# Score products one level later in TensorE's order, behind the making of the next level's operands, in a gated-linear-attention and mixture-of-experts block

## Chip, cores and metric

The kernel runs on one core of one Trainium2 chip. The metric is device time in microseconds (us); lower is better.

## What is computed

One decoder block over 512 tokens of width 1024, in fp32. A projection of the normalised input feeds a convolution branch and a chunked gated linear attention (GLA); both are gated, added and projected; a mixture of 32 experts (top 2) and a final norm follow. The part that the change touches is the intra-chunk score of the GLA:

```python
diff = b[:, :, :, None, :] - b[:, :, None, :, :]
decay = jnp.exp(jnp.where(causal, diff, -jnp.inf))
attn = jnp.einsum("bhid,bhijd,bhjd->bhij", qc, decay, kc)
o_intra = jnp.einsum("bhij,bhje->bhie", attn, vc)
```

with `b` the running sum of the log gates (4 heads of 128 keys and 256 values).

## The kernel before

TensorE is PE, VectorE DVE, ScalarE ACT, GpSimd POOL, SyncE SP. The 512 tokens stand in four blocks of 128. Every large product is done as three fp32r passes over high and low parts of its operands. The weights are streamed in pieces: `piece` loads one (SP), rounds it to a high part on ACT (`hiw`, `hipw`, `higo`, L410) and subtracts on POOL or DVE to get the low part (`low`, `lopw`, `logo`, L384).

`scores(t)` makes the score matrix of block `t` in seven levels, `l` = 0 to 6. At level `l` pairs of neighbouring groups of 2^l tokens meet. DVE makes the difference `dd` of `b` to a reference row in two instructions, ACT its exponential `fac` (one PSUM bank, tag `bg`), DVE the product tile `m` of `fac` with keys and with queries in two instructions, PE the product `pl` (small matmuls on halves of the array), and DVE (levels 0 to 4, `copy_predicated`) or ACT (levels 5 and 6) puts the valid part into `attn`. `dd` and `m` have two buffers each, `pl` two banks (tag `g`).

The program is written in the order: convolution, values (`tm`, token-major), scores 0 and 1, read gate `r` (`tm`), block 0, scores 2 and 3, blocks 1 to 3, normalisation and transposes, first branch gate (`fmw`, evacuated to `yc`), convolution output product (`pw`), second branch gate (`fmw`, evacuated to `th`), GLA output product (`fmgo`), output product (`wo`), router, experts. But in this part of the program the engines' orders (except SP's, and from `wo` on PE's, DVE's and ACT's) are not the written ones: a scheduler with a timeline of its own lays them out, with the dependencies and with the extra order hints of `after(ins, other)`, which make no instruction wait and only say that `ins` is to be placed no earlier than `other` is done on that timeline.

`block(t)` multiplies `attn` and the state with the values into `po` (two banks, tag `tr`), and carries the state on (`kd`, `pk`, `kt`, `pst`, `st`). After block 3 the squares give `so` (square root on ACT, reciprocal on DVE), 16 DVE instructions scale `sr` by it, and for k = 0 to 7 PE transposes `sr` into `pot` (tag `tr`, two banks), ACT rounds to the high part and DVE subtracts for the low part (`ohl`, `olo`, L69). `fmgo` sums over k = 0 to 7 in each of its eight tiles, so its first tile needs all eight of them.

In the background DVE sums rows of the modulation weights (`acc_a`, `acc_b`, twice `acc_ga`, `acc_bf`, `acc_af`, 8 instructions each) from 1 MB transfers that ACT's queue issues into two buffers (`aw_...`).

Of the kernel before, what the change touches and what calls it, by code (L numbers as in the profile page):

```python
# [25 lines left out]
H = 4  # L26
# [34 lines left out]
def kernel(ctx: ExitStack, tc: tile.TileContext, a, dbg=None):  # L61
# [3 lines left out]
    def tt(out, in0, in1, op):  # L65
        return V.tensor_tensor(out, in0, in1, op=op)  # L66
# [12 lines left out]
    def after(ins, other):  # L79
        tc.add_manual_dep(raw_ins(ins), raw_ins(other).name, NOSYNC, reason="order")  # L80
# [483 lines left out]
    def scores(t):  # L564
# [12 lines left out]
        bf = b.rearrange("p h i -> p (h i)")  # L577
        kf = kb[t].rearrange("p h i -> p (h i)")
        qf = qb[t].rearrange("p h i -> p (h i)")
        for l in range(7):  # L580
            s = 1 << l
            m = H * P // (2 * s)
            half = lambda x: x.rearrange("p (m g s) -> p m g s", g=2, s=s)
            dd = tl("dd", f"dd{t}_{l}")
            ref = half(bf)[:, :, 0, s - 1:s].to_broadcast([P, m, s])
            tt(half(dd)[:, :, 0, :], ref, half(bf)[:, :, 0, :], ALU.subtract)
            tt(half(dd)[:, :, 1, :], half(bf)[:, :, 1, :], ref, ALU.subtract)

            fac = bank("bg", f"fac{t}_{l}")
            A.activation(fac, dd, AF.Exp)  # L590
            mm = tl("mm", f"m{t}_{l}", (P, H, P))
            mf = mm.rearrange("p h i -> p (h i)")
            tt(half(mf)[:, :, 0, :], half(fac)[:, :, 0, :], half(kf)[:, :, 0, :], ALU.mult)
            tt(half(mf)[:, :, 1, :], half(fac)[:, :, 1, :], half(qf)[:, :, 1, :], ALU.mult)

            pl = bank("g", f"pl{t}_{l}")
            if l == 6:
                for h in range(H):
                    T.matmul(pl[0:64, h * 64:(h + 1) * 64], mm[:, h, sides[0]], mm[:, h, sides[1]], start=True, stop=True, tile_position=(0, 0))
                A.copy(at[0:64, :, sides[1]], pl[0:64, 0:H * 64].rearrange("p (h i) -> p h i", h=H))  # L600
                continue
            if l == 5:
                for h in range(H):
                    for e in range(2):
                        T.matmul(pl[64 * e:64 * e + 32, h * 32:(h + 1) * 32], mm[:, h, 64 * e:64 * e + 32], mm[:, h, 64 * e + 32:64 * e + 64],
                                 start=True, stop=True, tile_position=(0, 64 * e))
# [12 lines left out]
    vt = [tl("v", f"v{t}") for t in range(NT)]
# [946 lines left out]
```

## Time and profile before

| | us |
|---|---|
| median of 3 runs | 1013.49 (1012.28 to 1017.1) |
| profiled execution, its own time | 1016.07 |
| span of its trace | 1014.4 |
| PE busy | 953.9 (94%) |
| DVE busy | 556.2 (55%) |
| ACT busy | 339.5 (33%) |
| POOL busy | 184.0 (18%) |

The profiled execution is 1016.07 us long, 1.7 us more than its span, and 2.6 us above the median. Busy shares are averages over stages that have different limits; a stage is read by the waits in it.

### The profile page before, as it was taken

The page shows a single profiled execution, that of the slowest core. Times are in us where ns is not written, and L with a number is a line of the kernel's source. Part 1 is how long each engine was busy: PE and PEld are TensorE (multiplying, and loading weights), DVE is VectorE, ACT ScalarE, POOL GpSimd, SP SyncE. Part 2 cuts the span into 40 slices and gives each one's busy share as a digit, 9 for nine tenths or more (in the row PEclk, how much of TensorE's full clock was granted, in tenths as well). Part 3 has the DMA queues.
Part 4 walks back from the last instruction along what each step waited for, and adds up shares of the span by engine and source line. Part 5 has one row for each costly group of instructions (what it writes and reads, how often), then busy time and mean ns, then how long its engine had stood idle before and what let it go on. Part 6 is the DMA issues. An engine that isn't in the chain of part 4 may idle for free.

```text
span 1014.4 us, 13547 instructions
## 1 busy us (share of the span) xinstructions
PE 953.9 (94%) x5170; PEld 612.9 (60%) x5170; DVE 556.2 (55%) x1039; ACT 339.5 (33%) x689; POOL 184.0 (18%) x122
## 2 busy tenths in 40 slices
PE   7999999999989999899999999999989999899993
PEld 4778899888768887687764353534435344344431
DVE  6768899888885898974441232323213232222436
ACT  7656323374136554433861101110110101101114
POOL 5513433322321111411220000000000000000005
PEclk9999999998999999999999999999999999999997
DMA  9863223214852678639659999999999999999952
GB/s 281 231 167 84 84 85 103 79 48 146 270 187 64 206 229 291 194 104 394 269 227 421 421 421 421 420 420 421 420 423 420 421 421 419 421 420 421 419 222 85
DMA packets 114344, 283.94 MB, mean 280 GB/s; under 512 B 10691, under 2 KB 77995, under 8 KB 90212
## 3 DMA queue, kind: packets, MB, share of 16 engines
q1 hardware_dynamic: 104636, 252.21, 65.3%
q10 hardware_dynamic: 7624, 27.27, 7.7%
q0 software_dynamic: 2016, 3.56, 0.9%
q8 instruction: 42, 0.69, 0.3%
q14 instruction: 26, 0.21, 0.1%
HBM read 282.61 MB, written 4.19 MB: 283 GB/s over the span
## 4 chain that ended last, share of the span: by engine, by line
PE 50%; DMA 22%; issue 9%; DVE 9%; POOL 5%; ACT 2%; SPq 2%; POOLq 0%; DVEq 0%; ACTq 0%
DMA p_w<-in_w 16%; PE pog L1391 8%; PE hag L1361 7%; PE hbg L1361 7%; PE fmw L393 6%; PE pcg L1436 5%; POOL low L384 4%; PE fmgo L393 3%; PE pw L393 2%; DMA adaw<-in_w_ada 2%; PE wo L262 2%; DVE dd L66 2%; PE wo L264 1%; PE wo L263 1%; DMA raww<-in_w_in 1%
## 5 line engine op out<-in xcount | busy, mean ns | idle before, releaser
L384 POOL TENSOR_TENSOR low<-raww,hiw 128x1024 fp32r<-128x1024 f32 x36 | 91.2, 2534 | 213.3 <-ACT hiw L410 213.3
L69 DVE SCALAR_TENSOR_TENSOR conv<-z,cols,conv 128x511 f32<-128x511 f32 (+14 forms) x120 | 88.6, 739 | 5.5 <-ACT conv L482 1.8
L393 PE MATMUL fmw<-uhi,hiw 128*128 128x512 f32 x224 | 90.3, 403 | 1.3 <-ACT hiw L410 0.8
L393 PE MATMUL fmw<-uhi,low 128*128 128x512 f32 x224 | 91.0, 406 | 0.0
L393 PE MATMUL fmw<-ulo,hiw 128*128 128x512 f32 x224 | 90.4, 404 | 0.0
L69 DVE SCALAR_TENSOR_TENSOR pog<-pog,wslg,ga2r 128x512 f32<-128x512 f32 (+1 forms) x33 | 24.5, 742 | 95.2 <-PE pog L1391 88.8
L393 PE MATMUL tm<-low,uhi 128*128 128x256 f32 x256 | 73.2, 287 | 0.0
L393 PE MATMUL tm<-hiw,uhi 128*128 128x256 f32 x256 | 73.0, 289 | 0.0
L393 PE MATMUL tm<-hiw,ulo 128*128 128x256 f32 x256 | 72.8, 286 | 0.0
L1436 PE MATMUL pcg<-ohlg,backg 128*128 128x512 f32 (+1 forms) x264 | 67.5, 404 | 5.2 <-DVE hx L66 4.1
L410 ACT CAST hiw<-raww 128x1024 fp32r<-128x1024 f32 x44 | 46.0, 1046 | 75.4 <-issue 41.8
L1436 PEld LDWEIGHTS pcg<-ohlg,backg 128*128 128x128 f32 x264 | 46.7, 189 | 23.3 <-DVE hx L66 11.1
L66 DVE TENSOR_TENSOR hx<-hx,pcg 128x512 f32<-128x512 f32 (+1 forms) x84 | 53.2, 659 | 12.9 <-PE pcg L1436 12.4
L393 PEld LDWEIGHTS tm<-low,uhi 128*128 128x128 f32 x256 | 49.1, 192 | 0.9 <-issue 0.5
L393 PEld LDWEIGHTS tm<-hiw,uhi 128*128 128x128 f32 x256 | 48.8, 192 | 0.8 <-issue 0.5
L393 PEld LDWEIGHTS tm<-hiw,ulo 128*128 128x128 f32 x256 | 49.2, 192 | 0.1
L393 PEld LDWEIGHTS fmw<-uhi,hiw 128*128 128x128 f32 x224 | 42.4, 189 | 11.2 <-ACT hiw L410 0.9
L393 PEld LDWEIGHTS fmw<-ulo,hiw 128*128 128x128 f32 x224 | 42.5, 190 | 9.9
L393 PEld LDWEIGHTS fmw<-uhi,low 128*128 128x128 f32 x224 | 42.5, 190 | 9.7
L1412 ACT CAST ohlg<-pog 128x512 fp32r<-128x512 f32 (+1 forms) x33 | 18.9, 572 | 78.7 <-DVE pog L69 78.7
L66 DVE TENSOR_TENSOR dd<-b 128x256 f32<-128x256 f32 x56 | 32.5, 624 | 0.4 <-ACT fac L590 0.2
L590 ACT ACTIVATE fac<-dd 128x512 f32<-128x512 f32 x28 | 16.8, 601 | 42.3 <-DVE m L66 42.2
(506 smaller groups left out, 1887.7 us busy)
## 6 DMA issues: line engine op xcount, KB each, us to landing
p_w<-in_w SPq DMA_DIRECT2D x188, 1024.0 KB, 19.9
raww<-in_w_in SPq DMA_DIRECT2D x44, 512.0 KB, 4.0
adaw<-in_w_ada SPq DMA_DIRECT2D x32, 256.0 KB, 5.5
aw_ga<-in_w_ada ACTq DMA_DIRECT2D x8, 1024.0 KB, 5.1
aw_a<-in_w_ada ACTq DMA_DIRECT2D x4, 1024.0 KB, 7.6
aw_b<-in_w_ada ACTq DMA_DIRECT2D x4, 1024.0 KB, 5.1
aw_bf<-in_w_ada_f ACTq DMA_DIRECT2D x4, 1024.0 KB, 5.9
rawgo<-in_w_gla_o SPq DMA_DIRECT2D x8, 512.0 KB, 4.9
```

Source lines behind the costliest of these rows:

```text
L66: return V.tensor_tensor(out, in0, in1, op=op)
L69: return V.scalar_tensor_tensor(out, in0, scalar, in1, op0=op0, op1=op1)
L262: mm(o, ahi, bhi, start=first, stop=False)
L263: mm(o, ahi, blo, start=False, stop=False)
L384: (V if turn[0] % LO_EVERY < lo_v[0] else G).tensor_tensor(lo, raw, hi.bitcast(F32), op=ALU.subtract)
L393: ins = T.matmul(*args, **kw)
L410: copy = A.copy(hi, raw)
L590: A.activation(fac, dd, AF.Exp)
L1361: T.matmul(o[64 * e:64 * e + 64, :], xts[0][:, k, q * P + 64 * e:q * P + 64 * e + 64], w[wn, e, k // 4][:, k % 4, :], start=(k == 0), stop ...
L1391: T.matmul(o[64 * e:64 * e + 64, :], ht[:, f, 64 * e:64 * e + 64], w["w2", e, f // 2][:, f % 2, c0:c1], start=(f == 0), stop=(f == 3), til ...
L1412: A.copy(ohl[:, 0, c0:c1], prods[c])
L1436: T.matmul(o, back[z][:, t * P:(t + 1) * P], res[z][:, i, c0:c1], start=(z == qs[0] and i == 0), stop=(z == qs[-1] and i == 1))
```

## The change

`scores` is cut into `factors(l)`, which makes `dd`, `fac` and `m` of a level, and `level(l, behind)`, which does its products and puts them into `attn`. Level 0's factors come first; then for each level the factors of the next level are written ahead of its products, and the first product of level `l` gets an order hint: it is to be placed behind the last DVE instruction of the factors of level `l + 1`. No instruction is added or removed, and no tile has more or fewer buffers. For level 6 there is no hint.

```diff
-        for l in range(7):
+        half = lambda x, s: x.rearrange("p (m g s) -> p m g s", g=2, s=s)
+        mms = {}
+
+        def factors(l):
+
             s = 1 << l
             m = H * P // (2 * s)
...
+            return tt(hm[:, :, 1, :], hf[:, :, 1, :], half(qf, s)[:, :, 1, :], ALU.mult)
+
+        def level(l, behind):
+
+            s = 1 << l
+            mm = mms[l]
+            start = []
+
+            def product(*args, **kw):
+                ins = T.matmul(*args, start=True, stop=True, **kw)
+                if behind is not None and not start:
+                    after(ins, behind)
+                start.append(ins)
+
 
             pl = bank("g", f"pl{t}_{l}")
...
+        factors(0)
+        for l in range(7):
+            level(l, factors(l + 1) if l < 6 else None)
```

The scheduler lays out everything behind the first moved product anew: PE's rows differ from the first products of block 0's scores to the first rows of `wo`, and so do DVE's, ACT's and some of POOL's in between; SP's are the same. Three places follow.

PE in the first branch gate, levels 1 and 2 of block 2's scores (`fmw` is the gate's product, `pl` a level's product, `m` its operands). Before:

```order
L393 MATMUL fmw_1_3224<-ulo,hiw_1_3220 128x512
L613 MATMUL pl_1_2664<-m_1_2661 64x32 x8
L613 MATMUL pl_2_2683<-m_2_2680 64x32 x8
L393 MATMUL fmw_1_3224<-uhi,low_1_3221 128x512
L393 MATMUL fmw_1_3224<-uhi,hiw_1_3220 128x512
```

and now:

```order
L393 MATMUL fmw_0_3257<-uhi,low_0_3254 128x512
L607 MATMUL pl_1_2672<-m_1_2650 64x32 x8
L393 MATMUL fmw_0_3257<-uhi,hiw_0_3253 128x512
L393 MATMUL fmw_0_3257<-ulo,hiw_0_3253 128x512
L393 MATMUL fmw_0_3257<-uhi,low_0_3254 128x512
```

Level 2's products no longer stand directly behind level 1's: 20 rows of `fmw` lie between them now, and as many ahead of most other levels; while `tm` runs it is about 21 rows. In the same way the scores of block 3, which stood among the last rows of the first gate, now stand among the rows of `pw`, and the last rows of block 3's `po`, which had 42 of the 192 rows of the second gate ahead of them, have 141.

PE at the transposes `pot` (the third of them, number 3056). Before it stood in the second gate, `fmw`:

```order
L393 MATMUL fmw_1_3888<-ulo,hiw_1_3858 128x512
L731 MATMUL pot_3056<-ident,sr_1320 128x128
L731 MATMUL pot_3056<-ident,sr_1321 128x128
L731 MATMUL pot_3056<-ident,sr_1322 128x128
L731 MATMUL pot_3056<-ident,sr_1323 128x128
L731 MATMUL pot_3064<-ident,sr_1320 128x128
```

and now behind the first row of `fmgo`'s first tile (4030):

```order
L393 MATMUL fmgo_4030<-ohl_3039,higo_4002 128x512
L752 MATMUL pot_3056<-ident,sr_1320 128x128
L752 MATMUL pot_3056<-ident,sr_1321 128x128
L752 MATMUL pot_3056<-ident,sr_1322 128x128
L752 MATMUL pot_3056<-ident,sr_1323 128x128
L393 MATMUL fmgo_4030<-ohl_3039,higo_4002 128x512
L393 MATMUL fmgo_4030<-ohl_3039,logo_4003 128x512
L393 MATMUL fmgo_4030<-ohl_3047,higo_4002 128x512
```

Six of the eight transposes stand inside that tile now, three rows of `fmgo` between one and the next; before it was two of them.

DVE at the same place, the last low parts of the transposed rows. Before:

```order
L69 SCALAR_TENSOR_TENSOR ohl_3063<-pot_3064,gq,ohl_3063 128x512
L384 TENSOR_TENSOR low_1_3960<-raww_1_3957,hiw_1_3959 128x1024
L69 SCALAR_TENSOR_TENSOR acc_bf<-aw_bf_3967,cact,acc_bf 128x1024 x2
L69 SCALAR_TENSOR_TENSOR olo_3072<-pot_3073,gq,ohi_3071 128x512
L69 SCALAR_TENSOR_TENSOR olo_3081<-pot_3082,gq,ohi_3080 128x512
L384 TENSOR_TENSOR logo_4062<-rawgo_4059,higo_4061 128x1024
```

and now:

```order
L69 SCALAR_TENSOR_TENSOR ohl_3063<-pot_3064,gq,ohl_3063 128x512
L69 SCALAR_TENSOR_TENSOR acc_bf<-aw_bf_3926,cact,acc_bf 128x1024
L69 SCALAR_TENSOR_TENSOR olo_3072<-pot_3073,gq,ohi_3071 128x512
L69 SCALAR_TENSOR_TENSOR acc_bf<-aw_bf_3926,cact,acc_bf 128x1024
L69 SCALAR_TENSOR_TENSOR olo_3081<-pot_3082,gq,ohi_3080 128x512
L69 SCALAR_TENSOR_TENSOR acc_bf<-aw_bf_3963,cact,acc_bf 128x1024
L69 SCALAR_TENSOR_TENSOR olo_3090<-pot_3091,gq,ohi_3089 128x512
```

From the first `sr` of block 3 (`sr_1323<-sr_1323,po_0`) to the last `olo` DVE now has one row of `acc_ga` more, and two of `acc_bf`, two of `low` and one of `woraw` fewer; from there to the next `logo` but one (the fourth tile's) two rows of `acc_bf` more, and one of `acc_af` and one of `mlo` fewer.

## Rows read from the trace of the kernel before

**Rows 1.** The page: the span, the busy time of the engines, and what the transfers moved in 40 equal slices of 25.4 us.

```profile
span 1014.4 us, 13547 instructions
PE 953.9 (94%) x5170; PEld 612.9 (60%) x5170; DVE 556.2 (55%) x1039; ACT 339.5 (33%) x689; POOL 184.0 (18%) x122
GB/s 281 231 167 84 84 85 103 79 48 146 270 187 64 206 229 291 194 104 394 269 227 421 421 421 421 420 420 421 420 423 420 421 421 419 421 420 421 419 222 85
```

**Rows 2.** Busy time by stage: start and end in us, length, then PE, PEld (weight loads), DVE, ACT and POOL with their instructions, the granted clock, the busy share of the DMA engines, GB/s. The stages are scores 0 and 1 beside the read gate; the first branch gate with scores 2 and most of 3; the second branch gate; the GLA output product; the experts.

```profile
187.00:246.00 59.00, 52.66 (x531) 48.24 (x531) 51.34 (x115) 34.41 (x54) 15.45 (x7) 0.94 0.24 65
246.00:311.00 65.00, 59.89 (x430) 47.81 (x429) 53.35 (x89) 20.55 (x38) 21.42 (x10) 0.97 0.66 222
343.00:397.00 54.00, 54.00 (x255) 44.34 (x254) 51.17 (x63) 25.72 (x66) 11.25 (x5) 1.00 0.81 268
397.00:458.00 61.00, 54.67 (x243) 44.06 (x242) 49.21 (x56) 27.07 (x62) 14.39 (x8) 0.97 0.51 163
525.00:975.00 450.00, 434.80 (x2023) 192.44 (x2020) 130.49 (x300) 63.66 (x125) 14.08 (x14) 1.00 1.01 420
```

**Rows 3.** Who waited for whom on PE between 165 and 330 us: us in total, times, the longest.

```profile
PE pl L613 <- DVE m L66: 7.4, 8, 2.0
PE pl L613 <- DVE attn L615: 1.4, 1, 1.4
PE pl L599 <- DVE m L66: 0.8, 1, 0.8
```

**Rows 4.** The 5 us stretches with the lowest granted clock (the last column but two), as in rows 2.

```profile
230.00:235.00 5.00, 3.32 (x40) 3.07 (x41) 4.82 (x16) 1.53 (x3) 0.00 (x0) 0.76 0.14 43
235.00:240.00 5.00, 5.00 (x39) 4.73 (x38) 3.71 (x9) 2.15 (x4) 2.37 (x1) 0.56 0.11 19
280.00:285.00 5.00, 3.03 (x34) 2.49 (x31) 4.94 (x9) 2.25 (x4) 1.14 (x1) 0.88 0.47 184
285.00:290.00 5.00, 5.00 (x19) 4.00 (x18) 4.94 (x7) 0.56 (x1) 1.55 (x1) 0.78 0.91 310
```

**Rows 5.** The chain of waits, pieces on PE: start, length in us, what, and how many.

```profile
234.07 5.21 PE tm L393 x23
...
242.17 1.62 PE tm L393 x12
...
292.60 4.63 PE fmw L393 x19
```

**Rows 6.** PE in order of time: one level's products alone, and two levels' back to back (start, length, and the idle time ahead with what ended it).

```profile
196.07 0.66 PE L613 MATMUL pl<-m 128*64 128x32 f32 x16 [0.64 <-DVE m L66]
...
303.09 1.12 PE L613 MATMUL pl<-m 128*64 128x32 f32 x32
```

**Rows 7.** The variance of the convolution branch: its last sum on DVE and its product on PE; and on ACT the tanh of the read gate behind which the last copy into block 0's scores is placed.

```profile
201.81 0.69 DVE L66 TENSOR_TENSOR csq<-csq,sq 128x512 f32<-128x512 f32 x1
...
202.56 1.12 PE L641 MATMUL pvar<-csq,onesc 128*128 128x512 f32 x2 [0.74 <-DVE csq L66]
...
222.34 0.59 ACT L658 ACTIVATE th<-tm 128x512 f32<-128x512 f32 x1
```

**Rows 8.** PE in order of time: the last products of block 3.

```profile
358.72 0.59 PE L680 MATMUL po<-st,eb 128*128 128x256 f32 x2
```

**Rows 9.** DVE in order of time, from block 3's first `sr` to the last `olo`, and the busy time of that stretch.

```profile
362.23 0.68 DVE L66 TENSOR_TENSOR sr<-sr,po 128x512 f32<-128x512 f32 x1
363.17 1.23 DVE L384 TENSOR_TENSOR low<-raww,hiw 128x1024 fp32r<-128x1024 f32 x1 [0.26 <-issue]
...
366.30 1.24 DVE L69 SCALAR_TENSOR_TENSOR acc_ga<-aw_ga,cact,acc_ga 128x1024 f32<-128x1024 f32 x1
367.46 3.50 DVE L720 TENSOR_SCALAR sr<-sr,so 128x256 f32<-128x256 f32 x13
...
384.53 5.23 DVE L69 SCALAR_TENSOR_TENSOR acc_bf<-aw_bf,cact,acc_bf 128x1024 f32<-128x1024 f32 x4
...
403.92 1.23 DVE L66 TENSOR_TENSOR woraw<-woraw,ga1r 128x1024 f32<-128x1024 f32 x1 [2.06 <-DMA woraw<-in_w_out]
405.06 0.74 DVE L69 SCALAR_TENSOR_TENSOR olo<-pot,gq,ohi 128x512 fp32r<-128x512 f32 x1
362.00:406.00 44.00, 42.55 (x202) 34.24 (x201) 38.68 (x53) 22.02 (x40) 8.89 (x4) 1.00 0.79 269
```

**Rows 10.** The fourth tile of `fmgo`: its wait on PE, the DVE instructions ahead of it that took longest, and POOL beside one of them.

```profile
406.86 2.93 DVE L833 TENSOR_TENSOR lo_ga<-acc_ga,hi_ga 128x512 fp32r<-128x512 f32 x1
...
410.30 2.29 DVE L791 TENSOR_SCALAR acc_af<-aw_af,cact 128x1024 f32<-128x1024 f32 x1
...
419.14 2.89 DVE L66 TENSOR_TENSOR woraw<-woraw,ga1r 128x1024 f32<-128x1024 f32 x1 [0.68 <-DMA woraw<-in_w_out]
422.55 1.21 DVE L384 TENSOR_TENSOR logo<-rawgo,higo 128x1024 fp32r<-128x1024 f32 x1
423.82 0.80 PE L393 MATMUL fmgo<-ohl,logo 128*128 128x512 f32 x1 [4.89 <-DVE logo L384]
418.54 2.41 POOL L384 TENSOR_TENSOR wo<-woraw,wo 128x1024 fp32r<-128x1024 f32 x1 [6.50 <-ACT wo L770]
```

**Rows 11.** The same two DVE instructions (`dd`) beside a POOL instruction and without one, and that POOL instruction.

```profile
188.32 2.92 DVE L66 TENSOR_TENSOR dd<-b 128x256 f32<-128x256 f32 x2
...
195.84 0.75 DVE L66 TENSOR_TENSOR dd<-b 128x256 f32<-128x256 f32 x2
188.44 2.52 POOL L384 TENSOR_TENSOR low<-raww,hiw 128x1024 fp32r<-128x1024 f32 x1 [3.25 <-ACT hiw L410]
```

**Rows 12.** A background transfer: size, and us from issue to landing.

```profile
aw_bf<-in_w_ada_f ACTq DMA_DIRECT2D x4, 1024.0 KB, 5.9
```

More of the change, by code (lines that the diff above doesn't have):

```diff
@@ L579, in scores @@
         qf = qb[t].rearrange("p h i -> p (h i)")
-        for l in range(7):
+        half = lambda x, s: x.rearrange("p (m g s) -> p m g s", g=2, s=s)
+        mms = {}
+        def factors(l):
             s = 1 << l
             m = H * P // (2 * s)
-            half = lambda x: x.rearrange("p (m g s) -> p m g s", g=2, s=s)
             dd = tl("dd", f"dd{t}_{l}")
-            ref = half(bf)[:, :, 0, s - 1:s].to_broadcast([P, m, s])
-            tt(half(dd)[:, :, 0, :], ref, half(bf)[:, :, 0, :], ALU.subtract)
-            tt(half(dd)[:, :, 1, :], half(bf)[:, :, 1, :], ref, ALU.subtract)
+            hd, hb = half(dd, s), half(bf, s)
+            ref = hb[:, :, 0, s - 1:s].to_broadcast([P, m, s])
+            tt(hd[:, :, 0, :], ref, hb[:, :, 0, :], ALU.subtract)
+            tt(hd[:, :, 1, :], hb[:, :, 1, :], ref, ALU.subtract)
             fac = bank("bg", f"fac{t}_{l}")
             A.activation(fac, dd, AF.Exp)
[L591 to L594, printed above, removed]
+            mm = mms[l] = tl("mm", f"m{t}_{l}", (P, H, P))
+            hm, hf = half(mm.rearrange("p h i -> p (h i)"), s), half(fac, s)
+            tt(hm[:, :, 0, :], hf[:, :, 0, :], half(kf, s)[:, :, 0, :], ALU.mult)
+            return tt(hm[:, :, 1, :], hf[:, :, 1, :], half(qf, s)[:, :, 1, :], ALU.mult)
[8 more added lines that the diff above has]
+                start.append(ins)
             pl = bank("g", f"pl{t}_{l}")
@@ L598, in scores @@
                 for h in range(H):
-                    T.matmul(pl[0:64, h * 64:(h + 1) * 64], mm[:, h, sides[0]], mm[:, h, sides[1]], start=True, stop=True, tile_position=(0, 0))
+                    product(pl[0:64, h * 64:(h + 1) * 64], mm[:, h, sides[0]], mm[:, h, sides[1]], tile_position=(0, 0))
                 A.copy(at[0:64, :, sides[1]], pl[0:64, 0:H * 64].rearrange("p (h i) -> p h i", h=H))
-                continue
+                return
             if l == 5:
@@ L604, in scores @@
                     for e in range(2):
-                        T.matmul(pl[64 * e:64 * e + 32, h * 32:(h + 1) * 32], mm[:, h, 64 * e:64 * e + 32], mm[:, h, 64 * e + 32:64 * e + 64],
-                                 start=True, stop=True, tile_position=(0, 64 * e))
+                        product(pl[64 * e:64 * e + 32, h * 32:(h + 1) * 32], mm[:, h, 64 * e:64 * e + 32], mm[:, h, 64 * e + 32:64 * e + 64],
+                                tile_position=(0, 64 * e))
                 for e in range(2):
                     A.copy(at[64 * e:64 * e + 32, :, 64 * e + 32:64 * e + 64], pl[64 * e:64 * e + 32, 0:H * 32].rearrange("p (h i) -> p h i", h=H))
-                continue
+                return
             second = lambda x: x.rearrange("p h (m g s) -> p h m g s", g=2, s=s)[:, :, :, 1, :]
@@ L612, in scores @@
                 for e, es in enumerate(sides):
-                    T.matmul(pl[es, h * 32:(h + 1) * 32], mm[:, h, es], second(mm[:, :, es])[:, h], start=True, stop=True, tile_position=(0, 64 * e))
+                    product(pl[es, h * 32:(h + 1) * 32], mm[:, h, es], second(mm[:, :, es])[:, h], tile_position=(0, 64 * e))
             for es in sides:
```

## Prediction, made before the changed kernel had run

> **What bounds the kernel now.** I read first the page's busy times and slices [rows 1], then the busy time by stage [rows 2], then PE's waits and clock [rows 3, 4], and last DVE in order of time [rows 9, 10].
>
> The second half is a transfer stage: from 525 to 975 us the DMA engines are busy throughout at 420 GB/s [rows 2]. It begins when PE begins to free the weight buffers; in the two slices before it the transfers run at 269 and 227 GB/s, so they have filled what there is and wait [rows 1]. What the front part gains or loses until then therefore moves the end one for one, and nothing here touches the experts.
>
> In the front part PE is the engine to watch. It is busy 52.66 of 59 us beside scores 0 and 1, and 59.89 of 65 beside scores 2 and 3, so 6.3 + 5.1 = 11.4 us stand idle there; in the second gate nothing is idle, and in the GLA output product 61 - 54.67 = 6.3 us [rows 2]. The idle time at the scores is what the change is aimed at: PE stands at a level's first product until DVE has made its operands, 7.4 + 0.8 us of it by name, and 1.4 for a bank [rows 3]. There is a second price. Behind these stops the granted clock falls from 1.00 to 0.76 and 0.56, and to 0.88 and 0.78, that is, for part of the time from the 2.4 to the 1.2 GHz level [rows 4]; 23 `tm` matmuls took 5.21 us there, where 12 take 1.62, so 23 should take 3.1 [rows 5]. The clock missing in the four stretches is (0.24 + 0.44 + 0.12 + 0.22) x 5 = 5.1 us; part of it fell into idle time, so I take 4.5. Beside all this DVE is nearly full: 51.3 of 59 and 53.4 of 65 us, 51.2 of 54 in the second gate, and it is what PE waits for in the GLA output product, 4.9 us at one spot [rows 2, 10].
>
> **The change, part by part.** Nothing is computed more or less; no instruction waits for anything that it did not need before. What changes is what stands where.
>
> *The scores' waits.* Ahead of most levels PE has 20 or 21 rows of other work now. A `tm` row is 1.62 / 12 = 0.135 us at most and an `fmw` row 4.63 / 19 = 0.244 [rows 5], so 2.8 and 4.9 us lie between two levels, while DVE needs for a level four instructions of the `dd` and `m` kind and two copies, some 2.2 us by 0.75 for a pair of `dd` [rows 11] and as much for each other pair. So when PE comes to a level its operands should be there, and the 11.4 us with their 4.5 us of clock go: 15.9. Not all of it. The variance product now comes on PE with less idle time behind it, while the DVE sum it waits for ended at 201.81 + 0.69 and moves little [rows 7]: I add 1.1 us to its 0.74. And block 0's `po` now stands between the scores of blocks 0 and 1, and needs ACT's last copy into `attn`, which is placed behind a tanh that ran at 222.34 [rows 7]; PE, by adding up its rows, would be there at about 219.3 and the copy done about 221.3, for ACT has less ahead of it: 2.0 us more, with bounds of 0 and 3.6. Third, levels that stood back to back are apart: two alone take 2 x 0.66, the pair took 1.12 [rows 6], so 0.2 us for each of four pairs, 0.8 in all. The Trainium skill (TensorEngine Tiling (Array Packing), Key Properties) says that changing the tiling mode drains TensorE, which speaks against taking such pairs apart; the rows agree that it costs something, and price it at those 0.8 us. Sum: 15.9 - 1.1 - 2.0 - 0.8 = 12.0 us by which PE is earlier when it begins with `pw`. Bounds: 9 and 15.
>
> *Block 3 goes back.* The same hints push block 3's scores from the first gate into `pw`, and its last `po` from behind 42 to behind 141 of the second gate's 192 rows: 99 x 0.244 = 24 us later in PE's own work. Its end was 358.72 + 0.59 = 359.3 [rows 8]; now it is 359.3 + 24 - 12 = 371. What is late next is the chain behind it: squares and root on ACT, scaling, transposes and low parts, which all of `fmgo` needs. In PE's own work there were 150 rows of `fmw` behind the last `po` to hide this chain, 36 us; now there are 51, 12 us.
>
> *How long the chain is.* It is DVE's, from block 3's first `sr` at 362.23 to the end of the last `olo`, 405.06 + 0.74 = 405.8: 43.6 us, of which 38.4 were work (38.68 in the 44 us from 362 to 406, less what lies behind the last `olo`), 5.2 waiting [rows 9]. DVE has in it now one `acc_ga` more (1.24), two `acc_bf` fewer (5.23 / 4 = 1.31 each), two `low` fewer and one `woraw` fewer (1.23 each) [rows 9]: 38.4 + 1.2 - 2.6 - 2.5 - 1.2 = 33.3 us. Its waits I cannot read off; I count 2.2 us for a `low` whose high part ACT makes only when `fmw` frees its buffer, 1.5 for the root, and 0.7 for an `acc_bf` whose transfer, issued as soon as its buffer is free, needs 5.9 us [rows 12]: 4.4, with bounds of 0 and 8. So 37.7 us from 370 (the first bank of `po` is done a little ahead of the second): the last `olo` at 407.7, against 405.8 before. PE by its own work would want it at 405.8 - 12 = 393.8. It will stand in the first `fmgo` tile between transposes, for some 14 us in pieces, and **the 12 us are given back there.**
>
> *Behind it.* PE then has the same work up to the fourth tile as before: it asked for that tile's low part at 423.82 - 4.89 = 418.9, 13.1 us after the last `olo` [rows 10]; now 407.7 + 13.1 = 420.8. DVE had the `logo` done at 422.55 + 1.21 = 423.8, 18.0 us behind the last `olo`; it has two `acc_bf` more, an `acc_af` and an `mlo` (0.68) fewer, so +0.6, and would be done at 426.3 if it meets the same collisions and waits. Without those (2.93, 2.29 and 2.89 us for instructions that take 0.7, 0.75 and 1.23 undisturbed, and a wait of 0.68 [rows 10]) it is 6 us quicker, and PE sets the time. The fourth tile starts between 420.8 and 426.3; I take the middle, 423.6, against 423.8. From there on both kernels have the same work.
>
> So the sum is 1016.07 - 0.2, no change for the profiled execution. That stands 2.6 us above the median; against the median I say **1013 us**. The likeliest case's own range, with the bounds above (9 to 15 us at the scores, 0 to 8 in the chain, 420.8 to 426.3), is 1008.5 to 1018.5.
>
> **The rivals.**
>
> *A, the gain gets through.* If the chain is not what holds the first `fmgo` tile, because DVE, with nothing to wait for, runs it in much less than 33 us, or PE gains more than I count, PE keeps its 12 us: 1013.5 - 12 = 1001.5. For it: DVE's stretch of 43.6 us before was partly spaced by PE's placing of the transposes, and 8 of its rows are background sums. Against it: those rows are in DVE's order ahead of the `olo`, and 33 us of work do not fit between 370 and 394. Half of it, 1006 to 1008, comes with a chain 6 us shorter.
>
> *B, slower: DVE and POOL collide in the chain.* A pair of `dd` that takes 0.75 us took 2.92 when a POOL subtraction of 2.52 us had begun beside it, and ended with it [rows 11]. The Trainium skill (SBUF — State Buffer, Who interferes with whom) calls this a lock: DVE with two SBUF inputs and a reading POOL instruction exclude each other for a whole instruction. In the chain the scaling (16 instructions), two `sr`, the bias sums and `lo_ga` read from SBUF only, and POOL makes the first tile's `logo` and, behind the last `olo`, halves of `wo` there. Each meeting costs up to 2.2 us [rows 11]; three more than before make the chain 6.6 us longer, and all of it is exposed, since PE has no cover left: 1013 + 6.6 = 1019.6. It decides from about two and a half more meetings on. Against it: the chain before had such meetings too [rows 10], and they are in my 38.4.
>
> *C, the change doesn't do what it says.* DVE is nearly full beside the scores, so operands could be late for the new places too; if half of the 15.9 us stays, block 3 ends 8 us later, and the chain with it: about 1020. Against it: with the levels 2.8 to 4.9 us apart, DVE has more time per level than it needs.
>
> **How the numbers follow.** What a measurement of this kernel can tell from no change is about 0.5%, 5 us. My forecast, within it, 0.47; A 0.30, taken as faster; B 0.15 and C 0.08, both slower. The time is the forecast's, 1013. For 8 in 10 the range takes in A down to its full price (1001.5, so 1002) and B to its full price: 1002 to 1020.
>
> **What the profile would show.** Right: PE's idle time from 187 to about 295 falls from 11 to some 4 us, with no stretch below a clock of 0.9 there; the first gate ends some 16 us sooner (12, and 4 for what moved out of it); the last `po` ends near 371; PE waits 10 us or more in the first `fmgo` tile for `olo` or `ohl`, and the last `olo` ends within 4 us of 405.8. Wrong: the last `olo` by 398 (rival A); a long DVE scaling or `lo_ga` beside POOL (B); `pl` still waiting for `m` by more than 4 us (C).

## The result, and the profile after

The changed kernel takes 1020.54 us (median of 9 runs, 1017.66 to 1022.41) against 1014.72 us of the kernel before on the same chip: a ratio of 1.0057, 95% interval 1.0044 to 1.0070. It is slower by 0.57%, just beyond what a measurement can tell from no change, and half a microsecond outside the predicted range. Of the 7.5 us between it and the 1013 us of the prediction, 1.2 are the kernel before, whose median was 1013.49 us when the prediction was made. The profiled execution of the changed kernel took 1022.41 us, 1.9 above its median.

| | before | after |
|---|---|---|
| span of the profiled execution, us | 1014.4 | 1020.7 |
| PE busy, us | 953.9 | 958.4 |
| DVE busy, us | 556.2 | 555.5 |

Busy time by stage of the changed kernel (the columns of [rows 2]):

```profile
187.00:246.00 59.00, 56.37 (x553) 50.71 (x552) 51.94 (x108) 33.12 (x50) 17.63 (x8) 0.97 0.28 85
246.00:311.00 65.00, 58.85 (x377) 45.95 (x376) 52.63 (x83) 23.67 (x43) 18.37 (x9) 1.00 0.66 213
343.00:397.00 54.00, 48.91 (x232) 40.01 (x230) 41.53 (x62) 29.11 (x96) 7.96 (x4) 1.00 0.57 179
397.00:458.00 61.00, 54.43 (x228) 42.75 (x229) 59.46 (x64) 25.60 (x50) 16.86 (x5) 0.89 0.65 220
525.00:975.00 450.00, 435.55 (x2029) 193.12 (x2031) 127.61 (x296) 66.33 (x129) 14.39 (x15) 1.00 1.01 419
```

Against [rows 2] PE stands 2.6 us instead of 6.3 beside scores 0 and 1, but 6.2 instead of 5.1 in the stretch from 246 to 311, and 5.1 in the second gate, where nothing was idle. DVE has lost 10 us of work in the second gate (41.53 against 51.17) and got them back behind it (59.46 of 61, against 49.21). The transfer stage is what it was.

PE's waits by name, first from 165 to 330 us, then from 330 to 525 (us in total, times, longest):

```profile
PE pl L607 <- DVE attn L66: 3.1, 1, 3.1
PE pvar L662 <- DVE csq L66: 2.3, 1, 2.3
PE po L699 <- DVE sr L66: 1.6, 1, 1.6
...
PE pl L607 <- DVE m L66: 0.3, 1, 0.3
...
PE fmgo L393 <- ACT ohl L753: 3.6, 1, 3.6
PE fmgo L393 <- DVE logo L384: 2.7, 1, 2.7
PE pot L752 <- DVE ohl L69: 1.9, 1, 1.9
PE pot L752 <- DVE sr L741: 1.4, 1, 1.4
...
```

The waits at which the hint is aimed are gone: 0.3 us for `m`, where there were 7.4 and 0.8 [rows 3]. Others stand in their place: one for `attn`, one for `sr`, one three times as long for the variance (0.7 before), three at the transposes and the first `fmgo` tile, and one at the fourth, where 4.9 stood before [rows 10]. Behind three of the four longest the granted clock is low; behind the wait for `attn`, the second longest, it stays at 1.00:

```profile
200.00:205.00 5.00, 3.01 (x22) 2.06 (x23) 4.87 (x13) 1.46 (x3) 0.71 (x1) 0.78 0.37 105
205.00:210.00 5.00, 5.00 (x49) 4.83 (x49) 4.26 (x5) 4.32 (x5) 1.66 (x1) 0.87 0.02 3
275.00:280.00 5.00, 1.92 (x20) 1.33 (x19) 3.80 (x6) 0.63 (x1) 0.00 (x0) 1.00 0.74 270
280.00:285.00 5.00, 5.00 (x31) 3.86 (x27) 4.90 (x9) 0.60 (x1) 0.00 (x0) 1.00 0.59 210
395.00:400.00 5.00, 1.28 (x6) 0.96 (x6) 4.83 (x6) 2.70 (x4) 0.00 (x0) 0.74 0.75 265
400.00:405.00 5.00, 4.94 (x19) 3.60 (x17) 5.00 (x8) 2.30 (x4) 0.00 (x0) 0.58 0.85 282
425.00:430.00 5.00, 2.29 (x10) 1.69 (x9) 5.00 (x6) 2.67 (x6) 1.30 (x1) 0.81 1.02 381
430.00:435.00 5.00, 5.00 (x13) 3.84 (x13) 5.00 (x5) 2.44 (x8) 5.00 (x2) 0.50 0.75 254
```

Four marks on the way, PE and DVE in order of time: the first row of `pw`, block 3's last `po` [rows 8], the last `olo` [rows 9] and the fourth `fmgo` tile [rows 10].

```profile
302.53 0.39 PE L393 MATMUL pw<-yhi,hipw 128*128 128x512 f32 x1
377.02 0.59 PE L701 MATMUL po<-st,eb 128*128 128x256 f32 x2
411.90 0.73 DVE L69 SCALAR_TENSOR_TENSOR olo<-pot,gq,ohi 128x512 fp32r<-128x512 f32 x1
428.74 0.79 PE L393 MATMUL fmgo<-ohl,logo 128*128 128x512 f32 x1 [2.71 <-DVE logo L384]
```

`pw` began at 311.57 before. Ahead of it then stood block 3's `pd` and its levels 0 to 4, which PE does in 0.69 + 0.66 + 2 x 1.12 = 3.6 us and which now stand behind; so PE's own gain is 9.0 - 3.6 = **5.4 us**, where the prediction had 12.0. The last `po` ends at 377.6 (371 predicted), the last `olo` at 412.6 (407.7), the fourth tile starts at 428.7 (423.6).

Where the 6.6 us went is seen, for the greater part, at block 2's `attn`. DVE in order of time, and PE and POOL beside it:

```profile
264.91 3.37 DVE L69 SCALAR_TENSOR_TENSOR acc_a<-aw_a,cact,acc_a 128x1024 f32<-128x1024 f32 x1
...
276.10 2.60 DVE L69 SCALAR_TENSOR_TENSOR acc_b<-aw_b,cact,acc_b 128x1024 f32<-128x1024 f32 x2 [5.18 <-DMA aw_b<-in_w_ada]
278.62 0.87 DVE L66 TENSOR_TENSOR attn<-pd,ident 64x256 f32<-64x256 f32 x2
279.64 0.66 PE L607 MATMUL pl<-m 128*64 128x32 f32 x16 [3.08 <-DVE attn L66]
264.27 2.92 POOL L384 TENSOR_TENSOR low<-raww,hiw 128x1024 fp32r<-128x1024 f32 x1 [5.02 <-ACT hiw L410]
```

DVE stands 5.18 us at a background sum whose transfer has not landed, does two sums, and only then multiplies `pd` by the identity into `attn`; that frees the `g` bank that PE's next products need. `pd` had been ready since 271.3 (270.65 + 0.69). In the kernel before these rows stood the other way round on DVE:

```
L69 SCALAR_TENSOR_TENSOR acc_a_3389<-aw_a_3438,cact,acc_a_3389 128x1024 x2
L791 TENSOR_SCALAR acc_b_3518<-aw_b_3519,cact 128x1024
L66 TENSOR_TENSOR attn_2624<-pd_2626,ident 64x4x64 x2
L69 SCALAR_TENSOR_TENSOR acc_b_3518<-aw_b_3519,cact,acc_b_3518 128x1024
...
L69 SCALAR_TENSOR_TENSOR acc_b_3518<-aw_b_3559,cact,acc_b_3518 128x1024
```

and now:

```
L69 SCALAR_TENSOR_TENSOR acc_b_3518<-aw_b_3519,cact,acc_b_3518 128x1024
L720 COPY st<-pst_0_2604 128x256
L720 COPY st<-pst_1_2609 128x256
L69 SCALAR_TENSOR_TENSOR acc_b_3518<-aw_b_3559,cact,acc_b_3518 128x1024 x2
L66 TENSOR_TENSOR attn_2624<-pd_2626,ident 64x4x64 x2
```

The hint on PE's products made the scheduler lay out DVE anew too, and two sums of `acc_b`'s second transfer (3559) came ahead of `attn`. A milder form of this could be seen in the profile before:

```profile
264.22 2.98 DVE L69 SCALAR_TENSOR_TENSOR acc_a<-aw_a,cact,acc_a 128x1024 f32<-128x1024 f32 x2 [3.09 <-DMA aw_a<-in_w_ada]
...
267.77 0.86 DVE L66 TENSOR_TENSOR attn<-pd,ident 64x256 f32<-64x256 f32 x2
```

There DVE stood 3.09 us for a transfer of `acc_a` ahead of the same `attn`, which began 3.4 us after `pd` was ready (264.4). PE's 1.4 us for `attn` in [rows 3], which the prediction counted as a wait for a bank, ended 3.0 us behind it; how much of them was due to those sums is not shown.

### The profile page after: what moved, and what is told of

Read it like the earlier page. It is cut to its first block, busy times and chain, and to the rows that moved or that the text cites. A ratio compares the mean times of both kernels' runs of the same rounds, so it can differ in the third digit from the quotient of the medians.

```text
span 1020.7 us, 13527 instructions
## 1 busy us (share of the span) xinstructions
PE 958.4 (94%) x5170; PEld 611.1 (60%) x5170; DVE 555.5 (54%) x1039; ACT 340.7 (33%) x689; POOL 185.4 (18%) x122
## 3 DMA queue, kind: packets, MB, share of 16 engines
q0 software_dynamic: 2016, 3.56, 0.9%
## 4 chain that ended last, share of the span: by engine, by line
PE 49%; DMA 17%; issue 16%; POOL 8%; DVE 6%; ACT 2%; SPq 2%; POOLq 0%; ACTq 0%; DVEq 0%
DMA p_w<-in_w 12%; PE pog L1412 9%; PE hag L1382 8%; POOL low L384 7%; PE hbg L1382 7%; PE pcg L1457 5%; PE fmw L393 3%; PE fmgo L393 3%; PE pw L393 2%; DMA adaw<-in_w_ada 2%; PE wo L262 2%; PE wo L263 1%; PE wo L264 1%; DMA aw_ga<-in_w_ada 1%; PE gxg L1346 1%
## 5 line engine op out<-in xcount | busy, mean ns | idle before, releaser
L384 POOL TENSOR_TENSOR low<-raww,hiw 128x1024 fp32r<-128x1024 f32 x36 | 88.9, 2470 | 212.7 <-ACT hiw L410 212.7
L1433 ACT CAST ohlg<-pog 128x512 fp32r<-128x512 f32 (+1 forms) x33 | 18.9, 571 | 80.4 <-DVE pog L69 80.4
L66 DVE TENSOR_TENSOR dd<-b 128x256 f32<-128x256 f32 x56 | 29.8, 574 | 6.0 <-ACT fac L594 5.8
L1367 ACT CAST backg<-pbkg 128x512 fp32r<-128x512 f32 x16 | 9.4, 586 | 64.6 <-PE pbkg L1365 57.5
```

The source lines that it names most:

```text
L384: (V if turn[0] % LO_EVERY < lo_v[0] else G).tensor_tensor(lo, raw, hi.bitcast(F32), op=ALU.subtract)
L1433: A.copy(ohl[:, 0, c0:c1], prods[c])
```

## The experiments

Two theories stood at the start. **S and P**: PE's gain is cut to 5 us by that background sum (S), and what is left of it is lost since block 3, pushed back, lays bare DVE's chain from the last `po` to the last `olo` (P). **R**: the new layout of the read gate costs by itself (the variance's wait, block 0's `po`, the low clock behind them). Later a third came in, **Q**: the background sums in that chain are what sets it. Each ratio below is to the kernel before on the same chip (1013.8 us for 1 to 4, 1013.9 for 5 to 8, 1013.1 for 9 to 11). The two marks come from one profiled execution of each kernel. The scheduler lays out much anew after most edits, so that beside the row meant others move too; that is said where it matters.

| kernel | last `po` ends | last `olo` ends | time, us | ratio (95%) |
|---|---|---|---|---|
| before | 359.3 | 405.8 | 1014.7 | |
| changed | 377.6 | 412.6 | 1020.5 | 1.0057 (1.0044 to 1.0070) |
| 1: hint for blocks 0, 1 | 361.1 | 408.8 | 1016.0 | 1.0029 (1.0015 to 1.0043) |
| 2: hint for blocks 2, 3 | 366.7 | 408.5 | 1017.3 | 1.0037 (1.0024 to 1.0050) |
| 3: `acc_b` behind `attn` | 372.6 | 406.9 | 1015.6 | 1.0023 (1.0012 to 1.0035) |
| 4: sums behind the last `olo` | 375.5 | 407.1 | 1024.9 | 1.0109 (1.0092 to 1.0127) |
| 5: before, `pr_` in `mm` | 348.3 | 390.2 | 1014.5 | 1.0009 (0.9995 to 1.0023) |
| 6: changed, `pr_` in `mm` | 373.1 | 408.8 | 1017.8 | 1.0039 (1.0023 to 1.0055) |
| 7: 3 and 6 | 370.6 | 405.7 | 1015.5 | 1.0019 (1.0005 to 1.0033) |
| 8: 1, 3 and 6 | 347.0 | 387.3 | 1008.8 | 0.9952 (0.9936 to 0.9968) |
| 9: 8 without 6 | 361.5 | 406.2 | 1013.6 | 1.0003 (0.9991 to 1.0016) |
| 10: 8 without 3 | 358.7 | 398.7 | 1014.5 | 1.0017 (1.0005 to 1.0029) |
| 11: 8 and `csq` | 354.6 | 393.5 | 1015.9 | 1.0020 (1.0009 to 1.0030) |

### 1 and 2: the hint for half of the blocks

```diff
-                if behind is not None and not start:
+                if behind is not None and not start and t < 2:    # 1
+                if behind is not None and not start and t >= 2:   # 2
```

1: 

> The hint stands for blocks 0 and 1 alone. By the order that comes out, the read gate and the first gate up to block 2's scores are those of the changed kernel, the background sum that waits for its transfer ahead of block 2's attn included; but block 3's last po has 69 rows of the second gate ahead of it, not 141 (42 before). Theory P (the loss is the pushed-back block 3 and the DVE chain behind it, laid bare): last po 359.3 + 27 x 0.244 - about 4 = 362, last olo 34 to 38 us later at 396 to 400 or where DVE's own rows allow it, up to 404; PE waits in the first fmgo tile 4 us or less; 1010 to 1014 us, some 7 to 10 under the changed kernel. Rival R (the new read gate itself costs: the variance product's wait, block 0's po early, the lower clock behind them): it stays within 3 us of the changed kernel, 1018 to 1021.

2: 

> The hint stands for blocks 2 and 3 alone: the read gate is that of before, with its waits for m, and block 3's last po has 96 rows of the second gate ahead of it (54 more than before, 13.2 us). Theory P: PE gains some 3 us in the first gate, the last po ends near 359.3 + 13.2 - 3 = 369, the last olo 34 to 37 us later at 403 to 406; four background sums more than before stand ahead of the fourth tile's low part on DVE (34, not 30), 5 us: the fourth tile starts near 426, and the time is 2 to 4 us above before, 1016 to 1019. Rival R: with the old read gate the loss is gone, 1014 or less.

Both land between before and the changed kernel, so neither half alone is the loss. R falls by 2, where it wanted no loss and there is 0.37%; kernel 8 below, the fastest, also has the read gate of the changed kernel. In 1 neither theory is clearly right: by the ratios it lies 2.8 us under the changed kernel, just within the 3 us of R and far from the 7 to 10 of P. P also missed the last `olo` there: the last `po` was where it was expected (361.1), the last `olo` came 48 us behind it, not 34 to 38. DVE in order of time:

```profile
388.47 0.75 DVE L812 TENSOR_SCALAR acc_bf<-aw_bf,cact 128x1024 f32<-128x1024 f32 x1 [2.53 <-DMA aw_bf<-in_w_ada_f]
```

With block 3 early, the background sums and their transfers fill the chain, as they did in the kernel before (46.5 us from last `po` to last `olo` there). Across the first six kernels of the table the last `po` moves by 18 us and the last `olo` by 7. So something else than block 3 alone keeps the last `olo` near 406 us or later. That is where Q comes from. In 2 the time came out as expected, with the last `po` 2.3 us earlier than that (366.7) and the last `olo` 2.5 us later (408.5).

### 3: one background sum behind `attn`

```diff
+            held["pd", t] = tt(at[es, :, es], pd[es, ...
...
+                    ins = stt(acc, w[:, e], cact[:, k:k + 1], acc, ALU.mult, ALU.add)
+                    if name == "b2" and k2 == 1:
+                        after(ins, held["pd", 2])
```

> The changed kernel with one more order hint: the first background sum of acc_b's second transfer is laid behind block 2's attn<-pd on DVE. PE's and ACT's rows stay as in the changed kernel; on DVE five rows trade places with their neighbours. Theory S (step one of the prediction failed since this sum, which waits 5.2 us for its transfer, stood in DVE's order ahead of attn, and held PE): PE's wait of 3.08 us for attn near 279.6 goes, everything behind is 3 us earlier (last po 374.5, last olo 409.5, fourth fmgo tile 425.6), 1017 to 1018 us. Rival: the wait only moves to the next level's product, or DVE's chain does not begin earlier since it waits for background transfers; within 1 us of the changed kernel.

This is the clean one: PE's rows are word for word those of the changed kernel, and on DVE five rows trade places. The stage from 246 to 311 us:

```profile
246.00:311.00 65.00, 63.31 (x411) 49.83 (x410) 54.09 (x90) 25.42 (x46) 20.44 (x9) 1.00 0.66 218
```

DVE in order of time at block 2's `attn`, and PE's marks:

```profile
270.04 0.88 DVE L66 TENSOR_TENSOR attn<-pd,ident 64x256 f32<-64x256 f32 x2 [0.53 <-PE pd L574]
273.09 1.29 DVE L69 SCALAR_TENSOR_TENSOR acc_b<-aw_b,cact,acc_b 128x1024 f32<-128x1024 f32 x1 [2.17 <-DMA aw_b<-in_w_ada]
...
297.52 0.40 PE L393 MATMUL pw<-yhi,hipw 128*128 128x512 f32 x1
423.02 0.50 PE L393 MATMUL fmgo<-ohl,logo 128*128 128x512 f32 x1 [2.64 <-DVE logo L384]
```

DVE still waits for the transfer, but `attn` is ahead of it. PE stands 1.7 us in this stretch, not 6.2; `pw`, the last `po`, the last `olo` and the fourth tile all come 5.0 to 5.7 us sooner than in the changed kernel. S is shown. Its size depends on the execution: the changed kernel's profile lies 1.9 us above its median and this one's 1.3 below; by the ratios the row costs 3.4 us (0.57% less 0.23%), about what was expected, and in kernel 4, which has the changed kernel's order up to there, `pw` begins at 300.5, only 3.0 us behind this one. With S out of the way this kernel's profile is close to the one I predicted: gain at `pw` 10.4 us, last `po` 372.6 (371), last `olo` 406.9 (407.7), fourth tile 423.0 (423.6). Its time is still 0.23% above the kernel before.

### 4: the last background sums behind the last `olo`

```diff
+        held["olo"] = stt(oh[k][1], pt, gq[:, k:k + 1], ...)
...
+                    ins = V.tensor_scalar(acc, w[:, e], cact[:, 0:1], None, op0=ALU.mult)
+                    if name in ("bf", "af"):
+                        after(ins, held["olo"])
```

> The changed kernel with one more order hint: the first of the acc_bf and acc_af background sums is laid behind the last olo, so that six acc_bf sums (0.76 + 5 x 1.26 = 7.1 us) leave DVE's chain between block 3's last po and the last olo, and 25 background sums, not 32, stand ahead of the fourth tile's low part. Theory P (DVE's order sets the first fmgo tile and the fourth): last olo 6 to 7 us earlier, near 406; fourth tile 6 to 8 us earlier, near 421 to 423, where PE becomes the limit; 1013 to 1015 us. Rival K (what costs is PE's own: the low clock behind its stops, transposes one bank at a time, or ACT's high parts): the last olo moves by 2 us or less and the time by 2 us or less.

The marks moved the way P had them: the last `olo` 5.6 us earlier than in the changed kernel, of which 2.1 were there at the last `po` already, so that the edit itself brought some 3.5 where 6 to 7 were expected; the fourth tile at 420.9, and the last row of `fmgo` at 455.2 instead of 460.9. Yet the time rose, by the ratios by 5 us. The stage behind `fmgo`:

```profile
460.00:525.00 65.00, 57.74 (x318) 44.97 (x317) 33.39 (x88) 37.71 (x75) 14.24 (x8) 0.92 0.78 302
```

DVE and PE in order of time there:

```profile
457.83 2.61 DVE L69 SCALAR_TENSOR_TENSOR acc_af<-aw_af,cact,acc_af 128x1024 f32<-128x1024 f32 x2 [0.71 <-DMA aw_af<-in_w_ada_f]
...
471.28 0.17 DVE L66 TENSOR_TENSOR afc<-afc,cols 128x8 f32<-128x8 f32 x1 [7.96 <-ACT pr_af L833]
...
483.74 0.64 PE L1041 MATMUL plgb<-const,ones 128*128 128x36 f32 x2 [6.58 <-DVE const L1036]
```

The sums put off are due in the router stage: `acc_af` was summed until 460.4, DVE then stood 8.0 us at `afc` for the transposes and row sums that finish it, the scaling of `wo` and the router's constant stood behind that in its order, and PE waited 6.6 us for the constant. The chain can be made shorter this way, but put behind the last `olo` its sums come too late for the router stage.

### 5 to 7: another bank for the transposes that finish the sums

```diff
-                        o = bank("bg", f"pr_{name}{c}{z}")
+                        o = bank("mm", f"pr_{name}{c}{z}")
```

In kernel 3 DVE idles 10.1 us from 326.9 to 337.0, and `acc_ga` begins only at 351.9, released by PE's `pr_a`, which takes the one `bg` bank that `fac` uses during the scores. The edit is made to the kernel before (5), to the changed one (6), and to kernel 3 (7).

5: 

> The kernel before, with one edit: the transposes that finish the background sums acc_a, acc_b, acc_bf and acc_af (pr_...) take their PSUM bank from tag mm (three banks), not from bg, whose one bank fac also uses during the scores. By the order, acc_ga can begin sooner, block 3's last po has none of the second gate's rows ahead of it (42 before), and all transposes pot stand inside the second gate. Theory Q (the background sums, held up by that one bank until the scores are through and then laid into the chain from block 3 to the last olo, set the last olo, in the kernel before too): PE's waits in the first and fourth fmgo tile (0.8 and 4.9 us, and the low clock behind them) shrink, 1006 to 1010 us. Rival (the chain does not matter in the kernel before): within 2 us of before.

6: 

> The changed kernel with the same edit as the last one: pr_ in the mm banks. Block 3's last po has 95 of the second gate's rows ahead of it (141 without the edit), and seven background sums stand between it and the last olo, not eleven. The background sum ahead of block 2's attn stays, so PE loses its 2 to 5 us in the first gate. Theory Q: last po near 366, last olo near 366 + 30 = 396, no long wait in the first fmgo tile; 1010 to 1013 us. Rival P alone (it is the distance of block 3 that costs): the last olo follows the last po at the same 34 to 35 us, 400 to 401, and the time is 1012 to 1015.

7: 

> The changed kernel with the order hint that lays acc_b's second transfer behind block 2's attn, and with pr_ in the mm banks. The same order as the last one but for that hint. Theory S: PE keeps 3 to 5 us that the one without the hint loses in the first gate, and everything behind is as much earlier: 1005 to 1009 us. Rival: the stall in the first gate was a matter of one execution; the same time as the one without the hint.

All three miss their times. In 5 the last `olo` comes 15.6 us earlier than before, and PE's waits at the first tile are gone, but the time is the same, as the rival had it. The wait has moved on. The stages at the transposes and at the tiles behind them:

```profile
377.00:412.00 35.00, 33.35 (x154) 26.72 (x153) 29.61 (x25) 15.93 (x35) 9.55 (x5) 1.00 0.69 237
412.00:435.00 23.00, 18.60 (x75) 15.42 (x76) 21.77 (x23) 10.73 (x26) 5.97 (x3) 0.85 0.65 205
```

and PE's longest wait there:

```profile
PE pr_af L807 <- DVE acc_af L69: 5.7, 1, 5.7
```

DVE is full up to the fourth tile (21.77 of 23 us), and what it has not done by then PE waits for, under one name or another: `logo` before, `acc_af` here, and for 3.7 us in 6 and 7 `mhi`, which ACT makes from DVE's `yc`.

Of Q the first half holds: the bank held the sums back. `acc_ga` begins at 328.0 in 5 (336.8 before) and at 317.7 in 7 (351.9 in 3). The second half, that the sums set the last `olo`, is not shown. In 5 there are still 15 background sums between block 3's first `sr` and the last `olo` (12 before); block 3 itself is earlier, its last `po` by 11.0 us, its first `sr` (349.3) by 12.9. And in 6 and 7, where seven sums are left there and not eleven, the last `olo` follows the last `po` at 35.7 and 35.1 us, about as the rival P alone had it (35.0 in the changed kernel). For 6 the stretch from the first `sr` to the last `olo`, and DVE's longest wait in it:

```profile
373.55:408.80 35.25, 32.75 (x159) 25.80 (x158) 24.28 (x43) 20.00 (x44) 7.26 (x3) 1.00 0.58 190
394.95 1.61 DVE L69 SCALAR_TENSOR_TENSOR ohl<-pot,gq,ohl 128x512 fp32r<-128x512 f32 x2 [5.33 <-ACT ohl L753]
```

DVE works 24.3 of 35.3 us there and stands 5.3 for a high part whose transposes PE did at 393.4, behind rows of the second gate and without a wait: there it is PE's order that holds the chain up. In 6 and 7 block 3 stays late (373 and 371, not 366 and 361), and between 6 and 7 the `acc_b` hint is worth 2.3 us, less than expected, with intervals that overlap.

### 8 to 10: the three edits together, and each of two taken away

8 is the hint for blocks 0 and 1, with the edits of 3 and 6.

8: 

> As the last one, but the change's hint stands for blocks 0 and 1 alone: block 3's last po has 17 rows of the second gate ahead of it, and all transposes stand inside the second gate, so that nothing in the first fmgo tile is left to wait for. Theory (the scores' waits are worth some 9 us of PE's time, and with neither the stall nor the chain in the way they come through): 7 to 9 us under the kernel before with pr_ in the mm banks, though blocks 2 and 3 keep their own waits for m (some 5 us of it): so 3 to 5 us under it, 1003 to 1006 us. Rival (DVE is full and gives back elsewhere what PE saves): no faster than the kernel before with pr_ in the mm banks.

9: 

> The fastest kernel so far (hint for blocks 0 and 1, acc_b's second transfer behind block 2's attn, pr_ in the mm banks) without the last of its three edits: pr_ is back in the bank bg that fac uses. By the order, block 3's last po has 83 rows of the second gate ahead of it, not 17, and acc_ga begins later. Theory Q (the one bg bank holds the background sums back and lays them into the chain): the last olo comes 15 to 20 us later, near 403 to 408, PE waits 4 to 7 us in the fmgo tiles, and the time is 4 to 7 us over the fastest, 1013 to 1015. Rival (the bank is of no matter, the two hints make the gain): 1008 to 1010.

10: 

> The fastest kernel so far without the second of its three edits: acc_b's second transfer stands ahead of block 2's attn again. Theory S (a sum that waits for its transfer ahead of attn holds PE): PE's wait for attn in the first gate is back, with 2 to 5 us more idle time between 246 and 311 us, and the time is 2 to 4 us over the fastest, 1010.5 to 1013. Rival (DVE has slack behind it, so that a stall in the first gate is made up by the fmgo tiles): 1008 to 1010.

8 beats both kernels: 1008.8 us, 0.48% under before, and 5.7 us under 5, which has neither of the two order hints (nor the new written order of the factors, which by itself left PE's read gate as it was: kernel 2). From 187 to 311 us, where the scores' waits are, PE stands 5.8 us in 8 and 11.3 in 5, which is nearly the whole difference, though the layouts differ elsewhere too. How much of it is the hint on the scores and how much the `acc_b` hint is not shown, since no run has the bank and the `acc_b` hint without the hint on the scores. The first gate in 8, and the stage at the tiles:

```profile
246.00:311.00 65.00, 61.77 (x442) 48.79 (x441) 57.37 (x96) 26.06 (x47) 20.11 (x9) 1.00 0.63 210
412.00:435.00 23.00, 22.06 (x90) 17.66 (x89) 16.56 (x19) 9.09 (x25) 6.15 (x3) 0.89 0.58 187
```

DVE does 57.37 us of work in the first gate (52.17 in 5) and has only 16.56 of 23 us left to do at the fourth tile, and PE stands 0.9 us there, not 4.4. Without the bank (9) the last `olo` is back at 406 and PE waits 3.6 us for an `olo` in the first tile: slower than 8 by 0.5%. These are Q's numbers, but here too block 3 moves as much as the chain's end: its first `sr` comes 20.8 us later than in 8 (367.4 against 346.6), the last `olo` 18.9. Without the `acc_b` hint (10) it is slower by 0.65%, about twice what S had; its profiled execution, with a span of 1018.7, lies 5.9 us above its own median, so it shows more than the usual loss. The loss lies where S has it, in the first gate (stage, then PE's longest wait in it):

```profile
246.00:311.00 65.00, 55.23 (x352) 43.63 (x351) 53.04 (x82) 20.64 (x39) 17.40 (x9) 0.95 0.64 215
```

```profile
PE pl L607 <- DVE m L66: 5.3, 2, 3.5
```

PE stands 1.4 us for `attn` there, and behind it for the next levels' `m`. In 9 and 10 other rows move besides, so their differences to 8 are not the price of one row alone.

### 11: the variance's wait

```diff
+            ins = tt(hd[:, :, 0, :], ref, hb[:, :, 0, :], ALU.subtract)
+            if t == 0 and l == 5:
+                after(ins, held["csq"])
```

> The fastest kernel so far with one more order hint: the differences dd of block 0's level 5 are laid behind the last sum csq, which the variance product pvar waits for. By the order, pvar stands five rows earlier on PE and the scheduler lays the read gate out anew behind it (block 0's po behind block 1's scores again). Theory: PE's wait of 2.3 us for csq and the low clock behind it (1.7 us in the changed kernel's profile) go, 2 to 4 us less, 1005 to 1007. Rival: DVE is as full there as before, and PE waits for another operand or for csq again: 1008 to 1010.

A miss of both, at 0.7% over 8: PE still waits 2.4 us for `csq`, since `pvar` too was laid five rows earlier, and the rest was laid out worse (5.3 us of waits for `m` again). What the variance's wait costs stays open.

## Why the prediction was wrong, point by point

**What bounds the kernel: right.** From the fourth tile to the end there were 590.6 us before and 592.0 now; what the front part loses moves the end one for one, but for 1.4 us; the clock behind the fourth tile's wait can account for them: 0.81 and 0.50 from 425 to 435 now (3.5 us missing), where before there were 0.87 and 0.79 (1.7 us), two stretches that [rows 4] leaves out:

```profile
420.00:425.00 5.00, 1.18 (x3) 1.00 (x4) 5.00 (x5) 2.48 (x3) 1.33 (x2) 0.87 0.62 209
425.00:430.00 5.00, 5.00 (x21) 4.05 (x20) 5.00 (x4) 0.79 (x2) 2.19 (x1) 0.79 0.87 284
```

***The scores' waits*, 12.0 us with bounds of 9 and 15: this is the step that failed.** It came out at 5.4. Its aim was met (waits for `m` 0.3 us), and of the deductions block 0's `po` cost nothing at its place, where 2.0 were counted. But the variance's wait was 2.33 us, not 1.84, and had a low clock behind it (0.78 and 0.87, up to 1.75 us) where the prediction said there would be none; and the term for the background sums ahead of `attn` was missing altogether: 5.0 us between the two profiles, 3.4 by the ratios of kernel 3. With 5.0 these terms bring 12.0 down to 6.8; the last 1.4 us, which kernel 3 lacks as well, stay open. I worked out what DVE needs between two levels and looked up what PE's rows had become, but not what had come ahead of `attn` in DVE's new order, which could be read from the order before any run.

***Block 3 goes back*, +24 us: right.** 371 predicted with a gain of 12; 377.6 with a gain of 5.4, 372.6 with 10.4 (kernel 3): the same 24 each time.

***How long the chain is*, 37.7 us: right in sum, by two errors that cancel.** By the same count, from 1 us ahead of the last `po`'s end, it was 36.0 in the changed kernel and 35.3 in kernel 3. But DVE came to block 3's first `sr` 5.3 us later than counted, since three sums of `acc_ga` stood ahead of it and one waited for its transfer, which is S over again:

```profile
380.70 1.28 DVE L69 SCALAR_TENSOR_TENSOR acc_ga<-aw_ga,cact,acc_ga 128x1024 f32<-128x1024 f32 x1 [2.52 <-DMA aw_ga<-in_w_ada]
381.90 0.68 DVE L66 TENSOR_TENSOR sr<-sr,po 128x512 f32<-128x512 f32 x1
```

From there to the last `olo` it took 30.7 us, 30.2 of them work, where 33.3 of work and 4.4 of waiting were predicted. The gain was given back in the first `fmgo` tile as described: PE stands 5.1 + 3.4 us from 377 to 412, and the clock of 0.74 and 0.58 adds at most 3.4 us: up to 12 of the 14 predicted. What I had not seen is how much of the chain in the kernel before was background work: kernel 1, with block 3 back at 361, has its last `olo` only 3.8 us earlier than the changed kernel. What alone sets the last `olo` stays open (kernels 5 to 7).

***Behind it*: right.** The fourth tile came 16.1 us behind the last `olo`, in the changed kernel and in kernel 3 alike; 15.9 were predicted, as the middle between PE's 13.1 and DVE's 18.6. It was DVE that set it: PE stood 2.7 us for `logo`.

**The rivals.** A did not come. C's number was right, 1020 by way of a block 3 some 7 us late, and its cause was not: the operands `m` were in time. B's collisions did not lengthen the chain: there was one meeting in it, in which the scaling took 6.41 us beside POOL's `logo` (4.37 before). Ahead of the stall there was one too: `acc_a`, which frees the buffer for the late transfer, took 3.37 us beside POOL's `low`, and 1.27 in kernel 3. The Trainium skill (SBUF — State Buffer, Who interferes with whom) says that a DVE instruction with two SBUF inputs contends with a GpSimd instruction that reads SBUF, and that the order of issue decides which of the two is blocked; the trace agrees: POOL's began 0.6 us earlier, and the sum ended 1.1 us behind its end at 267.2. But this does not set the stall apart from the other executions: in kernel 3 the same `low` met the `kd` just ahead of `acc_a`, which took 2.86 us and not 0.67. What differs is the transfer. Issued at 268.3, it let DVE go on at 276.1, 7.8 us later; in kernel 3 it was 6.3, and 5.9 for the one in [rows 12].

**Of the signs** I listed, the first (idle time 11 to 4, and it was 8.8; no clock below 0.9, and it was 0.78), the gate's end (9.0 us sooner, not 16) and the last `po` told the failure at once; "still waiting for `m`", the sign for C, did not, and a wait for `attn` was on no list.

## What to carry to other kernels

Where a scheduler lays out the rows, an order hint on one engine moves the others' rows too: read the new order of every engine that feeds the one that waits, and look above all for rows that wait for a transfer and now stand ahead of something wanted. Work in the background is not free because it is early enough on average; in a full engine's order it decides when everything behind it comes, and here it could be neither put off (kernel 4) nor left to wait for a bank (kernel 9). When each of several edits alone gives nothing, try them together before dropping them: three that gave 1.0003 to 1.0039 in smaller sets gave 0.9952 here.

## What was not expected of the hardware

The stall had a size of its own in each execution: with the same DVE rows up to that point DVE waited 5.18 us for `acc_b`'s second transfer in the changed kernel, 3.38 in kernel 1 and 1.81 in kernel 4; from its issue to DVE's going on the transfer took 7.8, 6.9 and 5.6 us.

A wait can cost PE more than its length, but not always: behind the 3.56 us at the first `fmgo` tile and the 2.71 us at the fourth the granted clock was 0.58 and 0.50 over five microseconds, that is, nearly all of that time at the 1.2 GHz level, while behind the 3.08 us at `attn` it stayed at 1.00. Likewise PE stood 6.3 us from 187 to 246 us in the kernel before, at a clock of 0.94 [rows 2], and 6.4 us in kernel 5, at 1.00:

```profile
187.00:246.00 59.00, 52.63 (x544) 47.93 (x543) 53.11 (x117) 36.47 (x61) 17.31 (x8) 1.00 0.28 84
```

So the 4.5 us of clock that the prediction counted as the price of the scores' stops are not tied to the stops alone; what decides is not shown.
